# The startup's modulation in plain fp32, on four column tiles of the array

## The chip, the cores and the metric

The kernel runs on one core of a Trainium2 chip. The metric is device time in microseconds (us), from the first to the last instruction of the slowest core, here the only one; several runs are given by their median. The engines are PE (TensorE, matrix products), DVE (VectorE), ACT (ScalarE), POOL (GpSimd) and SP (SyncE, which here issues DMA transfers).

## What is computed

The program is a block of a hybrid model with three layers over 512 latent tokens and 256 context tokens, of width 2048. The change concerns the beginning of the first layer alone:

```python
shift_l, scale_l, gate_l = jnp.split(mod_lat, 3, axis=-1)
shift_c, scale_c, gate_c = jnp.split(mod_ctx, 3, axis=-1)
u_l = rms_norm(h_lat, pre_w) * (1 + scale_l[:, None]) + shift_l[:, None]
u_c = rms_norm(h_ctx, pre_w) * (1 + scale_c) + shift_c
z_l, xbc_l, dt_l, qkv_l, b_l, a_l = _split_proj(u_l @ w_in)
z_c, xbc_c, dt_c, qkv_c, b_c, a_c = _split_proj(u_c @ w_in)
```

`mod_lat` and `mod_ctx` are `silu(c) @ w_ada + b_ada` for two vectors of length 2048, one for the latent tokens and one for the context. Shift and scale are 4096 columns of `w_ada`, so 33.5 MB of weights are multiplied by two vectors only. The gate's columns are worked out elsewhere and are not touched.

## The kernel before, in words

Activations lie feature-major: 16 chunks of 128 features in the partitions, tokens in the columns. The large products run with split operands: a float32 value becomes a high part and a low part in a reduced format (`float32r`, F32R in the code), and three products (low weight by high activation, high by low, high by high) are added in PSUM. `gemm_steps` (L165 to L202) loads a block's weights four contraction chunks at a time (`wr`), converts them on ACT (`wh`, L183), subtracts on DVE (`wl`, L184), and issues the products at L198, contraction chunk by contraction chunk.

`startup` (L309) makes the input of the first layer. It has four inner steps:

- `modulation(k)` (L329) makes shift and scale of feature chunk k for both vectors. The stationary operand `c4` holds, for a contraction chunk, four columns: high and low parts of the two vectors. The moving operand is the weight, 128 x 256 for a contraction chunk (128 columns of shift, 128 of scale). It is loaded two contraction chunks at a time (`wa`, 256 KB, ten buffers), converted on ACT (`wah`, L336) and subtracted on DVE, every fourth time on POOL (`wal`, L337). So 32 products with a 4 x 256 result are added up in `pr` (L340). The sum is copied to `row` (ACT, L343), and two small fp32 products with `sel` (`pm`, L346) turn it into columns and add the parts; three DVE steps make `mod` (L350 to L352).
- `square(k)` (L355) loads chunk k of both streams (`raw`) and adds up their squares in `acc`.
- `rsqrt_rows` (L281) makes the norm's scale from `acc` (`rs`, L286).
- `modulate(k)` (L367) makes `u` on DVE (L372, L373) and splits it into `hi` (ACT, L274) and `xlo` (DVE, L275). These are the operands of all later products over chunk k.

`modulation(0)` and the sixteen squares come first; then, for each k, `modulation(k)` and `modulate(k)`. Beside them `phase_a` (L760) runs the first four blocks, over latent tokens (`mm`, 512 columns) and context (256 columns, shown as `s`): per chunk k these are 12 products of each kind, which can start when chunk k's `hi` and `xlo` are there.

The whole of this part is inside a block whose order a scheduler sets, from a model of its own; what it sets is a fixed order on each engine. Each engine, and SP's queue of transfers too, works it off strictly in that order. PSUM has two buffers for `pr`, `pm` and `rs` together while this runs.

Of the kernel before, what the change touches and what calls it, by code (L numbers as in the profile page):

```python
# [17 lines left out]
# products of other blocks between the dependent ones of the gated delta rule, by weight  # L18
# [4 lines left out]
# ---------------------------------------------------------------- layout on the host  # L23
# [107 lines left out]
# ---------------------------------------------------------------- the program  # L131
class Prog:
# [8 lines left out]
    # ---- constants  # L141
# [18 lines left out]
    # ---- products with split operands  # L160
# [4 lines left out]
    def gemm_steps(self, blocks, kc=16):  # L165
        """blocks: dicts of src [128, kc, M], acts [(hi, lo, psum ap)], done().  The blocks run
        together, contraction chunk by contraction chunk; a step is one matmul."""
# [36 lines left out]
    def gemm_tokens(self, src, done):  # L204
        """A product with the tokens in the partitions: src [128, 16, n], done(chunk of tokens, psum)."""
# [22 lines left out]
    def weave(self, steps, n, weight):  # L228
        """Steps of other products to place between dependent matmuls: n of them over the given weight."""
        self.steps, self.left, self.weight = steps, n, weight  # L230
# [10 lines left out]
    def run_slots(self, chain, other=None, skip=0, scale=1.0):  # L241
        """A chain of dependent products; between two of them a link of the other chain and steps of the filler."""
# [24 lines left out]
    # ---- small helpers  # L267
# [13 lines left out]
    def rsqrt_rows(self, acc, n, out, tmp):  # L281
        """out[p, t] = (sum_p acc[p, t] / n + eps) ** -0.5, the same in every partition."""
# [6 lines left out]
        # one table for both  # L289
# [3 lines left out]
        # one step of Newton's method  # L293
# [4 lines left out]
    def transposes(self, ps, dst, srcs):  # L298
        """PE transposes of srcs (each [a, b]) next to each other into one bank, one copy out."""
        nc = self.nc  # L300
        o = 0
        for s in srcs:
            a, b = s.shape
            nc.tensor.transpose(ps[:b, o:o + a], s, self.ident[:a, :a])
            o += a


    # ---- block 1, phase A: modulation, input projections of both streams, SSD, GDN preparation
    def startup(self):  # L309
        nc, D = self.nc, self.D  # L310
        self.xh, self.xl, self.ch, self.cl = [], [], [], []
        with self.tc.tile_pool(name="st", bufs=2, side="right") as st:
# [7 lines left out]
            nc.vector.tensor_scalar(out=cc, in0=cc, scalar1=0.5, scalar2=None, op0=MUL)  # L320
            # both vectors' high and low parts, next to each other as stationary columns
            c4 = st.tile([P, 16, 4], F32R, name="c4", bufs=1)
            nc.scalar.activation(out=c4[:, :, 0:2], in_=cc, func=AF.Copy)
            nc.vector.tensor_tensor(out=c4[:, :, 2:4], in0=cc, in1=c4[:, :, 0:2].bitcast(F32), op=SUB)  # L324
            sel = st.tile([4, 2], F32, name="sel", bufs=1)
            nc.vector.tensor_tensor(out=sel, in0=self.ident[0:4, 0:2], in1=self.ident[0:4, 2:4], op=ADD)
            xr, cr, R, mod = [], [], acc, st.tile([P, 16, 2, 2], F32, name="mod", bufs=1)

            def modulation(k):  # L329
                pr = self.sc("pr")  # L330
                for q in range(8):
                    w = st.tile([P, 2, 256], F32, name="wa", bufs=10)
                    nc.sync.dma_start(w, D["wada"][k, :, 2 * q:2 * q + 2])
                    wh = st.tile([P, 2, 256], F32R, name="wah", bufs=6)
                    wl = st.tile([P, 2, 256], F32R, name="wal", bufs=6)
                    nc.scalar.activation(out=wh, in_=w, func=AF.Copy)  # L336
                    (nc.gpsimd if q % 4 == 3 else nc.vector).tensor_tensor(out=wl, in0=w, in1=wh.bitcast(F32), op=SUB)  # L337
                    for j in range(2):
                        for i, x in enumerate((wl, wh)):
                            nc.tensor.matmul(pr[0:4, 0:256], c4[:, 2 * q + j, :], x[:, j, :],  # L340
                                             start=(q + j + i == 0), stop=(q + j + i == 9))
                row = st.tile([4, 256], F32, name="row")
                nc.scalar.activation(out=row, in_=pr[0:4, 0:256], func=AF.Copy)  # L343
# [11 lines left out]
            def square(k):  # L355
                # the streams wait in the places of their parts
# [24 lines left out]
            # the first modulations run beside the loads of the streams  # L381
# [13 lines left out]
    def conv_consts(self):  # L395
        """Half of the convolutions' taps and bias: silu(x) = (tanh(x / 2) + 1) * (x / 2)."""
# [22 lines left out]
    def conv5(self, ps, is_lat, taps, bias, out, th):  # L419
        """out = silu of the centred convolution of ps."""  # L420
# [20 lines left out]
    def both(self, src, done, share=None):  # L441
        """A block over the latent tokens and over the context."""
# [10 lines left out]
    def conv_block(self, names, j, has_bias, sink):  # L453
        """done() of a block that goes through a convolution; sink(out_lat, out_ctx)."""
# [16 lines left out]
    def small_done(self, ps, pc):  # L471
        """dt, beta and alpha of all tokens (context first): decays and their sums in each chunk."""
        nc, b1 = self.nc, self.b1
        with self.tc.tile_pool(name="sm", bufs=1, side="right") as st:
# [59 lines left out]
            # decay to the chunk's end times dt; minus the decay from the chunk's start  # L534
# [5 lines left out]
    # ---- SSD: units of four heads  # L540
# [3 lines left out]
    def ssd_bc(self, kind, lat, ctx):  # L544
        """B or C of a group: keep the feature-major latent part, B also token-major."""
# [12 lines left out]
    def to_tm(self, dst, lat, ctx, eng="act"):  # L558
        """dst[:, c, :] (token-major chunks) from feature-major latent and context parts."""
# [19 lines left out]
    def ssd_unit(self, u, xt):  # L579
        """Four heads; xt [tokens of a chunk, chunk, 256] holds their x."""  # L580
# [35 lines left out]
        # feature-major, to DRAM  # L616
# [40 lines left out]
    # ---- gated delta rule, preparation: everything that needs k and v alone  # L657
    def gdn_prep(self, h):
# [23 lines left out]
        # token-major k and its squared norms  # L682
# [19 lines left out]
        # token-major v over the norm of k  # L702
# [8 lines left out]
        # X[j, i] = k_j . k_i with the decay between j and i: forward above, backward below  # L711
# [9 lines left out]
        # its diagonal blocks of 32, rows scaled, lower triangular for both directions  # L721
# [16 lines left out]
    def gdn_solve(self, h, g, eng):  # L738
        """Inverses of the unit lower triangular 32-blocks of two heads, a block in a partition."""
# [6 lines left out]
        # in place: 2 on the diagonal turns the column of a step into its negative  # L746
# [13 lines left out]
    def phase_a(self):  # L760
# [74 lines left out]
        with tc.tile_pool(name="gp", bufs=1, side="right") as self.gp:  # L835
# [18 lines left out]
            # the first queries and gate, while the last preparations end  # L854
# [13 lines left out]
    # ---- gated delta rule: the inverses, the scans  # L868
    def gdn_data(self, h, hd):
        """What the scans of a head need."""  # L870
# [4 lines left out]
    def gdn_load(self, h):  # L875
        """The operands of the products for a head's inverses."""
# [35 lines left out]
    def gdn_merge(self, hd):  # L912
        """W = (I + D X)^-1 of every chunk (forward: upper, backward: lower), from its diagonal
        blocks; both directions share the products."""
# [11 lines left out]
        # 32 -> 64  # L926
# [13 lines left out]
        # 64 -> 128  # L940
# [17 lines left out]
    def gdn_step(self, h, hd, cs, S, tag, last=False):  # L958
        """One chunk of both directions' scans: the corrected values; the next states into S."""
# [47 lines left out]
    def gdn_lat(self, h, hd, qf, before):  # L1007
        """before: what takes the last head's outputs."""
# [11 lines left out]
        # squared norms of q  # L1020
# [34 lines left out]
        # the norms of q and of the outputs, token by token  # L1055
# [13 lines left out]
        return o  # L1069

    def zgate(self, ps, pool, pin=lambda ins: ins):
        """2 silu(z)."""
        nc = self.nc
        zs = pool.tile([P, 512], F32, name="zs")
        pin(nc.scalar.activation(out=zs, in_=ps, func=AF.Tanh, scale=0.5))
# [888 lines left out]
```

## Time and profile before

| | us |
|---|---|
| median of 3 runs | 3560.84 |
| lowest, highest | 3559.32, 3570.53 |
| span of the profiled execution | 3565.4 |

The time of the profiled execution is its span, 3565.4 us: one execution of its own, beside the three that were timed. The profile's views are: the page (busy time of each engine, and the span in slices); busy time by stretches of the span, with the granted TensorE clock as a share of full speed (1.00 is 2.4 GHz, 0.50 is 1.2 GHz) and the DMA engines' share; groups of instructions by line and shape, with count, busy time, mean of one in ns, and the engine's idle time just before them with what ended it; and instructions in order of time. A product in plain fp32 stands in the trace as two records of PE (and two weight loads, on the row PEld), one in `float32r` as one. The busy time of a record on PE goes on for a while after the next one has started, so that what a product occupies is read from start to start.

### The profile page before, as it was taken

The page shows a single profiled execution, that of the slowest core. Times are in us where ns is not written, and L with a number is a line of the kernel's source. Part 1 is how long each engine was busy: PE and PEld are TensorE (multiplying, and loading weights), DVE is VectorE, ACT ScalarE, POOL GpSimd, SP SyncE. Part 2 cuts the span into 40 slices and gives each one's busy share as a digit, 9 for nine tenths or more (in the row PEclk, how much of TensorE's full clock was granted, in tenths as well). Part 3 has the DMA queues.
Part 4 walks back from the last instruction along what each step waited for, and adds up shares of the span by engine and source line. Part 5 has one row for each costly group of instructions (what it writes and reads, how often), then busy time and mean ns, then how long its engine had stood idle before and what let it go on. Part 6 is the DMA issues. An engine that isn't in the chain of part 4 may idle for free.

```text
span 3565.4 us, 49253 instructions
## 1 busy us (share of the span) xinstructions
PE 3410.4 (96%) x17334; PEld 2843.3 (80%) x17334; DVE 2172.4 (61%) x4187; ACT 1511.4 (42%) x3036; POOL 543.6 (15%) x679
## 2 busy tenths in 40 slices
PE   5899999989999998999999999999999999999998
PEld 4688888878888786778888788887888888878887
DVE  7978776778865657666565634546444535353456
ACT  6554434444444435664333434434333333332334
POOL 4211114851110003202231201000000000000000
PEclk8999999999999999999999999999999999999999
DMA  8723336664443774333323454453333333345345
GB/s 272 239 78 108 92 83 215 205 193 133 126 127 94 231 250 137 101 113 95 98 83 98 116 183 136 136 149 107 107 105 101 101 102 102 89 132 156 96 123 170
DMA packets 293257, 479.79 MB, mean 135 GB/s; under 512 B 53689, under 2 KB 86841, under 8 KB 290833
## 3 DMA queue, kind: packets, MB, share of 16 engines
q1 hardware_dynamic: 293008, 476.65, 45.1%
q8 instruction: 136, 2.23, 0.3%
q14 instruction: 113, 0.92, 0.1%
HBM read 415.17 MB, written 61.34 MB: 134 GB/s over the span
## 4 chain that ended last, share of the span: by engine, by line
PE 72%; DVE 12%; DMA 7%; issue 3%; ACT 3%; POOL 2%; SPq 0%; DVEq 0%; ACTq 0%; POOLq 0%
PE mm L198 52%; PE mm L222 3%; PE mm L223 2%; PE mm L224 2%; PE mmc L198 2%; DVE wl L184 2%; DMA wg<-in_wgate 1%; PE pr L340 1%; DVE e L1570 1%; PE mg L922 1%; PE pl L198 1%; DMA araw<-yF 1%; ACT wh L183 1%; DVE at L1577 1%; PE s L198 1%
## 5 line engine op out<-in xcount | busy, mean ns | idle before, releaser
L198 PE MATMUL mm<-hi,wl 128*128 128x512 f32 (+2 forms) x3632 | 1414.7, 392 | 22.7 <-DVE wl L184 14.6
L198 PE MATMUL mm<-xlo,wh 128*128 128x512 f32 (+2 forms) x3632 | 1421.0, 391 | 6.4 <-DVE xlo L278 6.4
L198 PE MATMUL mm<-hi,wh 128*128 128x512 f32 (+2 forms) x3632 | 1415.1, 390 | 0.0
L184 DVE TENSOR_TENSOR wl<-wr,wh 128x512 fp32r<-128x512 f32 (+1 forms) x940 | 657.4, 705 | 687.0 <-ACT wh L183 683.1
L183 ACT ACTIVATE wh<-wr 128x512 fp32r<-128x512 f32 (+1 forms) x940 | 579.6, 621 | 1153.4 <-PE mm L198 908.0
L198 PEld LDWEIGHTS mm<-hi,wl 128*128 128x128 f32 (+1 forms) x3632 | 687.2, 190 | 149.2 <-DVE wl L184 19.9
L198 PEld LDWEIGHTS mm<-xlo,wh 128*128 128x128 f32 (+1 forms) x3632 | 686.6, 189 | 143.0 <-DVE xlo L278 8.7
L198 PEld LDWEIGHTS mm<-hi,wh 128*128 128x128 f32 (+1 forms) x3632 | 686.0, 189 | 122.8 <-issue 3.6
L222 PE MATMUL mm<-wl,hi 128*128 128x256 f32 (+1 forms) x512 | 172.3, 336 | 0.0
L223 PE MATMUL mm<-wh,xlo 128*128 128x256 f32 (+1 forms) x512 | 172.2, 336 | 0.0
L224 PE MATMUL mm<-wh,hi 128*128 128x256 f32 (+1 forms) x512 | 172.0, 336 | 0.0
L216 ACT ACTIVATE wh<-wr 128x512 fp32r<-128x512 f32 x96 | 60.6, 632 | 156.5 <-PE mm L224 77.7
L217 DVE TENSOR_TENSOR wl<-wr,wh 128x512 fp32r<-128x512 f32 x96 | 68.4, 714 | 88.9 <-ACT wh L216 88.4
L436 DVE SCALAR_TENSOR_TENSOR cvl<-padl,hc,cvl 128x512 f32<-128x512 f32 x112 | 91.8, 827 | 24.7 <-ACT cvl L432 15.5
L198 PE MATMUL mmc<-xlo,wh 128*128 128x256 f32 x368 | 106.0, 288 | 0.0
L222 PEld LDWEIGHTS mm<-wl,hi 128*128 128x128 f32 x512 | 97.2, 190 | 10.4 <-DVE pad L1349 0.3
L198 PE MATMUL mmc<-hi,wl 128*128 128x256 f32 x368 | 105.4, 286 | 0.0
L198 PE MATMUL mmc<-hi,wh 128*128 128x256 f32 x368 | 105.3, 286 | 0.0
L223 PEld LDWEIGHTS mm<-wh,xlo 128*128 128x128 f32 x512 | 97.2, 190 | 10.0
L224 PEld LDWEIGHTS mm<-wh,hi 128*128 128x128 f32 x512 | 97.2, 190 | 10.0
L340 PE MATMUL pr<-wal,c 128*4 128x256 f32 x256 | 69.4, 300 | 23.7 <-DVE c L324 10.6
L336 ACT ACTIVATE wah<-wa 128x512 fp32r<-128x512 f32 x128 | 74.5, 620 | 39.7 <-PE pr L340 23.7
(588 smaller groups left out, 4406.1 us busy)
## 6 DMA issues: line engine op xcount, KB each, us to landing
wr<-in_o_in SPq DMA_DIRECT2D x192, 256.0 KB, 3.1
wr<-in_e_in SPq DMA_DIRECT2D x160, 256.0 KB, 3.1
wr<-in_pgate SPq DMA_DIRECT2D x148, 256.0 KB, 3.3
wa<-in_wada SPq DMA_DIRECT2D x128, 256.0 KB, 4.2
wr<-in_w_qkv SPq DMA_DIRECT2D x96, 256.0 KB, 3.2
wr<-in_w_z SPq DMA_DIRECT2D x64, 256.0 KB, 3.1
wr<-in_w_out SPq DMA_DIRECT2D x64, 256.0 KB, 4.5
wg<-in_wgate SPq DMA_DIRECT2D x16, 1024.0 KB, 7.5
```

What stands on the lines that cost most here:

```text
L183: nc.scalar.activation(out=hi, in_=r, func=AF.Copy)
L184: nc.vector.tensor_tensor(out=lo, in0=r, in1=hi.bitcast(F32), op=SUB)
L198: nc.tensor.matmul(ap, w[:, kk, :], x, start=(n == 0), stop=(n == total[key] - 1))
L216: nc.scalar.activation(out=hi, in_=r, func=AF.Copy)
L217: nc.vector.tensor_tensor(out=lo, in0=r, in1=hi.bitcast(F32), op=SUB)
L222: nc.tensor.matmul(ps[c][:, :n], self.xh[k][:, t], lo[:, i], start=first, stop=False)
L223: nc.tensor.matmul(ps[c][:, :n], self.xl[k][:, t], hi[:, i], start=False, stop=False)
L224: nc.tensor.matmul(ps[c][:, :n], self.xh[k][:, t], hi[:, i], start=False, stop=last)
L336: nc.scalar.activation(out=wh, in_=w, func=AF.Copy)
L340: nc.tensor.matmul(pr[0:4, 0:256], c4[:, 2 * q + j, :], x[:, j, :], start=(q + j + i == 0), stop=(q + j + i == 9))
L436: nc.vector.scalar_tensor_tensor(out=ov, in0=pad[:, :, j:j + n], scalar=taps[j], in1=ov, op0=MUL, op1=ADD)
L922: nc.tensor.matmul(v[:, c], lhs[:, c], rhs[:, c], start=True, stop=True)
```

## The change

Inside `startup` only. Conversion and subtraction of the weights are left out, and with them `wah`, `wal` and the split of the two vectors. The vectors lie in `c32`, padded with zeros to 32 columns, in plain fp32. Weights are loaded four contraction chunks at a time (512 KB, ten buffers), and each of the four is multiplied in its own 32 columns of the array (`tile_position=(0, 32 * j)`), with its result in its own 32 partitions of `pr`. Per feature chunk there are 16 products with a 32 x 256 result. `row` then has 128 partitions, and `sel` adds the four partial sums: it has ones in rows 0, 32, 64 and 96 for the first vector, and in the rows after those for the second.

```diff
-            nc.vector.tensor_scalar(out=cc, in0=cc, scalar1=0.5, scalar2=None, op0=MUL)
-            c4 = st.tile([P, 16, 4], F32R, name="c4", bufs=1)
-            nc.scalar.activation(out=c4[:, :, 0:2], in_=cc, func=AF.Copy)
-            nc.vector.tensor_tensor(out=c4[:, :, 2:4], in0=cc, in1=c4[:, :, 0:2].bitcast(F32), op=SUB)
-            sel = st.tile([4, 2], F32, name="sel", bufs=1)
-            nc.vector.tensor_tensor(out=sel, in0=self.ident[0:4, 0:2], in1=self.ident[0:4, 2:4], op=ADD)
+            c32 = st.tile([P, 16, 32], F32, name="c32", bufs=1)
+            nc.gpsimd.memset(c32, 0.0)
+            nc.vector.tensor_scalar(out=c32[:, :, 0:2], in0=cc, scalar1=0.5, scalar2=None, op0=MUL)
+            sel = st.tile([P, 2], F32, name="sel", bufs=1)
+            s01 = st.tile([P, 2], F32, name="s01", bufs=1)
+            nc.vector.tensor_tensor(out=sel, in0=self.ident[:, 0:2], in1=self.ident[:, 32:34], op=ADD)
+            nc.vector.tensor_tensor(out=s01, in0=self.ident[:, 64:66], in1=self.ident[:, 96:98], op=ADD)
+            nc.vector.tensor_tensor(out=sel, in0=sel, in1=s01, op=ADD)
...
             def modulation(k):
                 pr = self.sc("pr")
-                for q in range(8):
-                    w = st.tile([P, 2, 256], F32, name="wa", bufs=10)
-                    nc.sync.dma_start(w, D["wada"][k, :, 2 * q:2 * q + 2])
-                    wh = st.tile([P, 2, 256], F32R, name="wah", bufs=6)
-                    wl = st.tile([P, 2, 256], F32R, name="wal", bufs=6)
-                    nc.scalar.activation(out=wh, in_=w, func=AF.Copy)
-                    (nc.gpsimd if q % 4 == 3 else nc.vector).tensor_tensor(out=wl, in0=w, in1=wh.bitcast(F32), op=SUB)
-                    for j in range(2):
-                        for i, x in enumerate((wl, wh)):
-                            nc.tensor.matmul(pr[0:4, 0:256], c4[:, 2 * q + j, :], x[:, j, :],
-                                             start=(q + j + i == 0), stop=(q + j + i == 9))
-                row = st.tile([4, 256], F32, name="row")
-                nc.scalar.activation(out=row, in_=pr[0:4, 0:256], func=AF.Copy)
+                for q in range(4):
+                    w = st.tile([P, 4, 256], F32, name="wa", bufs=10)
+                    nc.sync.dma_start(w, D["wada"][k, :, 4 * q:4 * q + 4])
+                    for j in range(4):
+                        nc.tensor.matmul(pr[32 * j:32 * j + 32, 0:256], c32[:, 4 * q + j, :], w[:, j, :],
+                                         start=(q == 0), stop=(q == 3), tile_position=(0, 32 * j))
+                row = st.tile([P, 256], F32, name="row")
+                nc.scalar.activation(out=row, in_=pr[:, 0:256], func=AF.Copy)
```

The scheduler sets the order anew. On PE, before, the products of a later modulation stand in pairs of low and high weights between those of the four blocks; here is the place behind a modulation's `pm` where the last of them are split up (`wal` and `wah` are the low and high weights, `c_109` the vectors, `s_...` the context's products):

```order
L198 MATMUL s_1959<-hi,wl 128x256
L340 MATMUL pr<-wal,c_109 4x256
L340 MATMUL pr<-wah,c_109 4x256
L340 MATMUL pr<-wal,c_109 4x256
L340 MATMUL pr<-wah,c_109 4x256
L198 MATMUL mm<-xlo,wh 128x512
```

And in the changed program, behind a `pm` near the same place (here L339 is the product and L345 `pm`):

```order
L345 MATMUL pm<-sel,row 128x2 x2
L339 MATMUL pr<-wa,c_108 32x256 x8
L198 MATMUL mm<-xlo,wh 128x512
L339 MATMUL pr<-wa,c_108 32x256 x4
L198 MATMUL mm<-hi,wh 128x512
L198 MATMUL s_1064<-xlo,wh 128x256
```

The products of a modulation now stand in groups of 4 to 16 between those of the blocks; over all sixteen modulations there are 27 such groups instead of 43.

On DVE, before, the subtractions stand between the steps of a chunk:

```order
L350 TENSOR_SCALAR mod<-pm,vec 128x2 x2
L372 TENSOR_TENSOR u<-raw,acc 128x256
L337 TENSOR_TENSOR wal<-wa,wah 128x512 x2
L352 TENSOR_SCALAR mod<-mod,vec 128x2
L337 TENSOR_TENSOR wal<-wa,wah 128x512
L373 TENSOR_SCALAR u<-u,mod 128x512
L373 TENSOR_SCALAR u<-u,mod 128x256
L337 TENSOR_TENSOR wal<-wa,wah 128x512
L275 TENSOR_TENSOR xlo<-u,hi 128x512
```

And in the changed program:

```order
L349 TENSOR_SCALAR mod<-pm,vec 128x2 x2
L351 TENSOR_SCALAR mod<-mod,vec 128x2
L372 TENSOR_SCALAR u<-u,mod 128x512
L372 TENSOR_SCALAR u<-u,mod 128x256
L275 TENSOR_TENSOR xlo<-u,hi 128x512
L275 TENSOR_TENSOR xlo<-u,hi 128x256
L371 TENSOR_TENSOR u<-raw,acc 128x512
L371 TENSOR_TENSOR u<-raw,acc 128x256
```

The steps that make `mod`, `u` and `xlo` of a chunk now follow each other directly.

## Rows read from the trace of the kernel before

**Rows 1.** The page: span, and busy time of each engine.
```profile
span 3565.4 us, 49253 instructions
PE 3410.4 (96%) x17334; PEld 2843.3 (80%) x17334; DVE 2172.4 (61%) x4187; ACT 1511.4 (42%) x3036; POOL 543.6 (15%) x679
```

**Rows 2.** Busy time by stretches (two answers of this view).
```profile
core 0: us, PE busy (x) PEld busy (x) DVE busy (x) ACT busy (x) POOL busy (x), PEclk, DMA share, GB/s
38.00:206.00 168.00, 150.80 (x930) 113.57 (x931) 144.90 (x251) 98.35 (x194) 50.20 (x42) 0.90 0.63 201
0.00:38.00 38.00, 7.67 (x37) 3.67 (x37) 22.64 (x36) 26.77 (x51) 17.91 (x28) 0.79 0.96 327
206.00:400.00 194.00, 190.27 (x1087) 166.25 (x1086) 160.71 (x361) 87.17 (x192) 26.49 (x30) 0.99 0.37 103
...
38.00:50.00 12.00, 8.66 (x44) 4.59 (x44) 10.67 (x14) 11.74 (x23) 4.75 (x4) 0.78 0.93 324
```

**Rows 3.** Order of time, PE, 60 to 84 us: start, length, instruction, count.
```profile
63.93 0.60 PE L346 MATMUL pm<-sel,row 4*128 4x2 f32 x4
64.46 0.28 PE L340 MATMUL pr<-wal,c 128*4 128x256 f32 x1
64.58 0.28 PE L340 MATMUL pr<-wah,c 128*4 128x256 f32 x1
...
73.06 0.39 PE L198 MATMUL mm<-xlo,wh 128*128 128x512 f32 x1
73.29 0.40 PE L198 MATMUL mm<-hi,wh 128*128 128x512 f32 x1
...
74.55 0.28 PE L198 MATMUL s<-hi,wh 128*128 128x256 f32 x1
74.67 0.28 PE L198 MATMUL s<-hi,wl 128*128 128x256 f32 x1
```

**Rows 4.** Groups by line and shape, 38 to 206 us.
```profile
L336 ACT ACTIVATE wah<-wa 128x512 fp32r<-128x512 f32 x120 | 69.4, 619 | 37.6 <-PE pr L340 23.7 <-issue 13.8
L337 DVE TENSOR_TENSOR wal<-wa,wah 128x512 fp32r<-128x512 f32 x90 | 65.1, 743 | 6.7 <-ACT wah L336 6.7
L340 PE MATMUL pr<-wah,c 128*4 128x256 f32 x240 | 63.4, 296 | 0.0
L340 PE MATMUL pr<-wal,c 128*4 128x256 f32 x240 | 63.4, 295 | 10.3 <-DVE wal L337 7.8 <-POOL wal L337 2.1 <-DVE sq L288 0.4
L337 POOL TENSOR_TENSOR wal<-wa,wah 128x512 fp32r<-128x512 f32 x30 | 48.3, 1612 | 103.9 <-ACT wah L336 97.1 <-DMA wa<-in_wada 6.8
...
L198 PE MATMUL mm<-hi,wl 128*128 128x512 f32 x65 | 21.1, 451 | 3.9 <-ACT hi L274 3.9
L198 PE MATMUL s<-xlo,wh 128*128 128x256 f32 x64 | 18.3, 292 | 0.8 <-DVE xlo L275 0.8
...
L275 DVE TENSOR_TENSOR xlo<-u,hi 128x512 fp32r<-128x512 f32 x16 | 17.4, 1086 | 3.2 <-ACT hi L274 2.9
...
L346 PE MATMUL pm<-sel,row 4*128 4x2 f32 x60 | 9.8, 265 | 2.2 <-DVE u L372 2.2
```

**Rows 5.** Order of time, PE, 37 to 62 us.
```profile
37.87 2.93 PE L286 MATMUL rs<-acc,ones 128*128 128x512 f32 x4 [16.41 <-DVE acc L365]
...
50.02 0.38 PE L340 MATMUL pr<-wal,c 128*4 128x256 f32 x1 [0.54 <-DVE wal L337]
50.20 0.41 PE L340 MATMUL pr<-wah,c 128*4 128x256 f32 x1
50.41 0.41 PE L340 MATMUL pr<-wal,c 128*4 128x256 f32 x1
```

**Rows 6.** Groups by line and shape: 300 to 3500 us, and PE over the span.
```profile
L275 DVE TENSOR_TENSOR xlo<-araw,hi 128x512 fp32r<-128x512 f32 x48 | 32.3, 687 | 18.2 <-ACT hi L274 18.2
...
L1025 PE MATMUL qn<-ones,sqq 128*128 128x1 f32 x64 | 7.6, 240 | 0.0
```

**Rows 7.** Order of time, all engines, 83 to 93 us.
```profile
87.03 3.91 POOL L337 TENSOR_TENSOR wal<-wa,wah 128x512 fp32r<-128x512 f32 x2 [5.08 <-ACT wah L336]
...
88.28 2.80 DVE L373 TENSOR_SCALAR u<-u,mod 128x512 f32<-128x512 f32 x2
...
88.41 0.28 PE L340 MATMUL pr<-wal,c 128*4 128x256 f32 x1 [0.66 <-DVE wal L337]
...
89.56 0.28 PE L340 MATMUL pr<-wal,c 128*4 128x256 f32 x1 [0.52 <-POOL wal L337]
```

**Rows 8.** Order of time, PE, 2508 to 2512 us: products in plain fp32, two records each.
```profile
2509.22 0.60 PE L1854 MATMUL nm<-vt,Wm 128*128 128x257 f32 x2
2509.65 0.59 PE L1860 MATMUL cm<-vt,kw 128*128 128x257 f32 x2
2510.09 0.60 PE L1856 MATMUL nm<-C,qg 128*128 128x257 f32 x2
```

**Rows 9.** Order of time, PE, 196 to 208 us.
```profile
199.84 2.07 PE L198 MATMUL mm<-hi,wl 128*128 128x512 f32 x4 [1.95 <-ACT hi L274]
...
202.14 0.63 PE L198 MATMUL mm<-xlo,wh 128*128 128x512 f32 x1
202.56 0.63 PE L198 MATMUL mm<-hi,wh 128*128 128x512 f32 x1
```

**Rows 10.** DMA queues, 38 to 206 us.
```profile
DMA packets 18534, 33.69 MB, mean 201 GB/s; under 512 B 2164, under 2 KB 2164, under 8 KB 18519
```

## The prediction

> **What bounds the kernel now.** I read the page first: PE is busy 96% of the span, nothing else over 61% [rows 1]. So the time moves by the work taken from PE or given to it, and by the idle time around it. The change touches only `startup`; with line and buffer numbers set aside, the order of the instructions after it is the same in both programs. So the second view is the busy time by stretches [rows 2]. The first 38 us belong to the DMA queues (share 0.96, 327 GB/s), and PE is busy 7.7 us in them. From 206 us on PE is busy 190.3 of 194 us at a granted clock of 0.99: whatever the startup ends earlier or later comes out at the end nearly whole. Between lies a stretch of 168 us (38 to 206) in which the 15 remaining modulations and the first four blocks' products run. There PE shows as busy 150.8 us, but at a mean clock of 0.90, and DVE is busy 144.9.
>
> What PE's work of that stretch is worth at the full clock I add up from starts in the order of time [rows 3]: a `pr` product each 0.116 us, a 512-column product each 0.23, a 256-column one each 0.116, the four records of `pm` 0.53. The groups [rows 4] give the counts: 480 x 0.116 = 55.7 for `pr`, 194 x 0.23 = 44.6, 192 x 0.116 = 22.3, 15 x 0.53 = 8.0, and 2.9 for the row sums `rs` [rows 5]. That is 133.5 of 168 us: **34.5 us are lost**. Idle before PE's groups makes 17.2 of it (10.3 + 3.9 + 2.2 + 0.8) [rows 4], and a clock 10% below full over 168 us makes 16.8, so the loss is accounted for. The low clock follows the idle: at 50.2 us, behind an idle 0.54, the same `pr` products start 0.21 us apart [rows 5], which is the 1.2 GHz level.
>
> Who causes the loss stands beside it. The 90 subtractions `wal` on DVE take 65.1 us, the 30 on POOL 48.3 [rows 4]. DVE's order puts them between the steps that turn a modulation into the next products' operands, and while POOL subtracts, DVE slows down: `xlo` of 128x512 has a mean of 1086 ns here against 687 later [rows 4, 6]. At 87 us POOL takes 3.91 us for two subtractions, two of DVE's `u` take 2.80 in the same time, and PE waits for both [rows 7].
>
> **The change, part by part.** The conversions `wah` (ACT, 120 in the stretch, 69.4 us) and the subtractions go away [rows 4]. They were on the path only where PE waited for them, so I count those waits and not their length. Loading stays 2 MB per chunk, in 64 transfers of 512 KB instead of 128 of 256. On SP the same 2 MB stand ahead of the stream's loads as before, so the squares and `rs` stay near 38 us: 0. The ten buffers now hold two and a half chunks instead of one and a quarter; the next weights of `w_xbc` queue behind them on SP, but are wanted only every four chunks: 0. The added memset (POOL) and the added sums for `sel` (DVE) lie before the first weights land: 0, and under 1 us without that cover. `row` keeps its 256 columns: 0. `pm` keeps two products, now over 128 rows instead of 4; fp32 records over 128 rows with one column have a mean of 240 ns, those of `pm` 265 [rows 4, 6]: 0.
>
> The `pr` products are the question. Per chunk, 32 one-record products become 16 in plain fp32, and the trace has no product in column tiles. The nearest are fp32 products of 257 columns over the whole array: two records each, one product every 0.43 to 0.44 us [rows 8]. From both sides: if the tiles share nothing, 240 x 0.435 = 104.4 us; if four run at once, a quarter, 26.1. I take the middle way, **two at once**: the two records of one product need the same columns of the array, and records start in program order [rows 8], so the second record of tile j can overlap only with the first of tile j+1. That is 0.2175 per product, 240 x 0.2175 = 52.2 us.
>
> Then the edges. The order has `pr` in 27 groups, 26 of them in this stretch. A group's last record runs alone: 26 x 0.22 = 5.7 us at least. If the array also has to empty on both sides, a record's length beyond the start of the next comes on top, 0.39 - 0.23 = 0.16 us [rows 3], twice: 26 x 0.54 = 14.0. I take the middle, 9.9. The Trainium skill ("TensorEngine Tiling (Array Packing)", Key Properties) says that changing the tiling mode drains TensorE, which speaks against the change; by it alone the edges cost the upper 14.0 and the gain below is 16 us. No row of this trace shows such a switch.
>
> So `pr` takes 52.2 + 9.9 = 62.1 instead of 55.7: PE gets 6.4 us more work. The gain must come from the 34.5 us lost. What stays: the slow clock of the first 12 us (0.78, 2.6 us) [rows 2], the wait for the last chunk's `hi` at 199.8 us (2.0) with the half clock after it (about 1.5) [rows 9], `xlo` 0.8, and about 1 for what is next in line, the chain `row`, `pm`, `mod`, `u`, `hi`, `xlo` of each chunk (some 3.5 us, covered by the next chunk's `pr` and the products of the chunk before). I keep 8. Gain: 34.5 - 8 - 6.4 = **20 us**; the startup ends at 186 instead of 206.
>
> DVE is no new bound: without `wal` it has 144.9 - 65.1 = 79.8 us, less without POOL beside it. DMA neither: 33.7 MB [rows 10], at the 327 GB/s of the first stretch are 103 us, done by 141.
>
> The sum is against the profiled execution, whose span is 3565.4 us; the median of the runs is 3560.84, 0.13% lower. I take the 20 us from the median: 3541.
>
> **Rivals.** *The tiles do not overlap* (slower). Then each product costs 0.435 and `pr` 104.4 + 26 x 0.16 for one emptying per group = 108.6, 52.9 more than now. With PE so full some 6 of the 34.5 stay lost: 52.9 - 28.5 = +24, 3585 us. It decides from the point where a chunk's `pr` costs, with its edges, 5.5 us instead of today's 3.7: 55.7 plus the 26.5 to be regained, over 15. My forecast has 62.1 / 15 = 4.1. For it: every fp32 product in the trace takes four times a split one, and no row shows two at once. Against: the tiles' outputs and weights are apart.
>
> *All four tiles run at once.* Then `pr` takes 26.1 + 9.9 = 36 us and PE is done after 77.8 + 36 + 8 = 122 us, at 160; the last weights land at 141, plus some 10 for the last chunk's chain and products. Both are close and will wait for each other a little: 160 to 166, a gain of 43, 3518 us. For it: four tiles, four outputs. Against: two records per product on the same columns. The Trainium skill ("TensorEngine Tiling (Array Packing)", Theoretical Speedup) gives up to 4 times for 32 columns, which would be this case.
>
> *Nothing to measure.* The second record also waits for its tile's weights to be loaded, so a chunk's `pr` costs 4.8 to 6.2 us with its edges and the regained waits pay for it: 15 x 0.7 = 10.5 us on either side of the point of decision above, 3550 to 3571.
>
> **How the numbers follow.** Two at once 0.50; none 0.23; four 0.15; in between 0.12. The measurement can tell about 0.3% from no change, 10.7 us. Of the first case a tenth falls within that, of the last most: faster 0.61, same 0.14, slower 0.25. The first case's own range is 3530 to 3552 (edges 5.7 to 14.0, kept losses 4 to 12, `rs` some us either way). To leave out no more than 2 in 10 the range must reach both other cases: 3516 to 3586.
>
> **What would show it.** Starts of consecutive `pr` records in the profile after: two records on the same start or at 0.11 us on average mean two tiles at once; 0.21 means none; 0.05 means four. The first four blocks' last 256-column products should end near 186 us; POOL nearly empty between 45 and 186; `xlo` of 128x512 near 690 ns; the granted clock there at 0.97 or more; no wait on `wal`. I am wrong if `pr` costs well over 4.1 us per chunk, or if PE keeps waiting though its work is the same: for `wa` from the DMA queues, or with the clock at the lower level inside the groups of `pr`.

## The result and the profile after

The change takes 3509.47 us, median of 4 runs (3507.06 to 3510.70), beside 3562.34 of the kernel before (3559.32 to 3570.53): ratio 0.9849, 95% interval 0.9837 to 0.9861. That is 52.9 us less. The prediction said 3541 in a range of 3516 to 3586: the sign is right, the size is not, and the range misses it. The profiled run has a span of 3508.2 against 3565.4 [rows 1].

The page after, its span and busy times. PE has 39 us less to do than in [rows 1], DVE 83, ACT 69, POOL 52:

```profile
span 3508.2 us, 48716 instructions
PE 3371.2 (96%) x17334; PEld 2813.7 (80%) x17334; DVE 2089.4 (60%) x4092; ACT 1442.6 (41%) x2907; POOL 491.2 (14%) x648
```

Where the startup ends shows where the time came from. The last `s` record starts at 205.5 us in the trace before and at 149.3 in that after, 56.2 earlier; the spans differ by 57.2. So nearly all of it lies ahead of that mark. The two records, first before, then after:

```profile
205.54 0.28 PE L198 MATMUL s<-hi,wh 128*128 128x256 f32 x1
```

```profile
149.27 0.28 PE L198 MATMUL s<-hi,wh 128*128 128x256 f32 x1
```

Busy time after, from the same 38 us to that mark, and the stretch of 194 us behind it, against [rows 2]:

```profile
core 0: us, PE busy (x) PEld busy (x) DVE busy (x) ACT busy (x) POOL busy (x), PEclk, DMA share, GB/s
38.00:149.50 111.50, 109.84 (x929) 80.37 (x928) 64.67 (x161) 34.10 (x72) 1.69 (x12) 1.00 0.80 298
149.50:343.50 194.00, 190.09 (x1064) 165.51 (x1063) 159.18 (x356) 84.81 (x188) 27.50 (x30) 0.97 0.37 101
```

As many records of PE (929 against 930) now lie in 111.5 us instead of 168, with 1.7 us of PE not busy where there were 17.2, and a mean granted clock of 1.00 where it was 0.90. DVE is busy 65 us instead of 145, POOL 1.7 instead of 50.

PE's groups of that stretch after, by line and shape (busy us, mean ns | idle before them), which answer to [rows 4]:

```profile
L339 PE MATMUL pr<-wa,c 128*32 128x256 f32 x480 | 32.0, 391 | 0.0
L198 PE MATMUL mm<-xlo,wh 128*128 128x512 f32 x64 | 26.2, 409 | 0.0
L198 PE MATMUL mm<-hi,wl 128*128 128x512 f32 x65 | 20.3, 401 | 0.6 <-ACT hi L274 0.6
L198 PE MATMUL s<-xlo,wh 128*128 128x256 f32 x64 | 18.0, 284 | 0.0
L345 PE MATMUL pm<-sel,row 128*128 128x2 f32 x60 | 7.6, 232 | 1.1 <-ACT row L342 1.1
```

The 480 `pr` records are 240 fp32 products of two records each. They were to cost 62.1 us and take 32.0. How they run shows in the order of time on PE after, some groups from 39 to 70 us (start, length, instruction, count); before stand [rows 3, 5]:

```profile
39.96 2.64 PE L339 MATMUL pr<-wa,c 128*32 128x256 f32 x32
...
47.56 0.50 PE L198 MATMUL mm<-xlo,wh 128*128 128x512 f32 x1
...
54.69 1.93 PE L339 MATMUL pr<-wa,c 128*32 128x256 f32 x32
56.55 0.39 PE L198 MATMUL s<-hi,wl 128*128 128x256 f32 x1
...
59.92 1.07 PE L339 MATMUL pr<-wa,c 128*32 128x256 f32 x16
60.93 0.50 PE L198 MATMUL mm<-xlo,wh 128*128 128x512 f32 x1
61.36 0.64 PE L339 MATMUL pr<-wa,c 128*32 128x256 f32 x8
61.93 0.50 PE L198 MATMUL mm<-hi,wh 128*128 128x512 f32 x1
```

From the first start of a group to the start of the next instruction, 32 records take 1.86 us, 16 take 1.00, 8 take 0.57: **0.432 us for four products (eight records), and 0.137 once per group**. The view groups like records, so the single starts of one group, read from the trace, stand here (us):

```
68.021 68.028 68.035 68.041 | 68.261 68.268 68.275 68.281 | 68.477 68.484 68.490 68.497 | 68.693 ...
```

Four records start within 20 ns, and 0.216 us later the next four: 0.054 on average. All four tiles run at once. These are the first records of the four products, then their four second records, since records of one tile start at least 0.216 apart in every run below.

The first 3.5 us of the window still run at half pace: `rs` takes 2.90 us, as long as before (2.93), and in the `x32` group at 39.96, which takes 2.64 us against 1.93 later, the starts of one tile are 0.427 us apart at first and 0.216 from 41.6 us on; the group at 44.24 runs at the later pace. (The view shows a granted clock of 1.00 from the first microsecond of this trace on, where the trace before shows 0.79 for the first 38 us [rows 2]. For these first microseconds I therefore go by starts.) Once the startup runs, PE shows no wait of note: 0.6 us for `hi`, 1.1 for `row`, both ahead of 46 us, and none for the DMA queues.

The other signs, in DVE's group after, 38 to 152 us, beside 1086 ns in [rows 4], and in the DMA queues of that stretch, beside [rows 10] (a digit is the share of one of 40 slices; below it GB/s):

```profile
L275 DVE TENSOR_TENSOR xlo<-u,hi 128x512 fp32r<-128x512 f32 x16 | 11.1, 692 | 5.2 <-ACT hi L274 5.2
```

```profile
DMA  9999999999589999999949999997796991000000
GB/s 414 405 410 398 408 408 408 410 397 398 207 234 369 355 362 395 417 411 401 359 128 231 395 346 406 413 411 277 234 341 201 285 353 64 0 0 0 0 1 6
DMA packets 10080, 33.23 MB, mean 292 GB/s; under 512 B 1228, under 2 KB 1228, under 8 KB 10068
```

The queues move 398 to 414 GB/s in the first 28 us, not 327, and the weights have landed near 135 us.

### The profile page after: what moved, and what is told of

Its sections match the earlier page's. It is cut to its first block, busy times and chain, and to the rows that moved or that the text cites. A ratio compares the mean times of both kernels' runs of the same rounds, so it can differ in the third digit from the quotient of the medians.

```text
span 3508.2 us, 48716 instructions
## 1 busy us (share of the span) xinstructions
PE 3371.2 (96%) x17334; PEld 2813.7 (80%) x17334; DVE 2089.4 (60%) x4092; ACT 1442.6 (41%) x2907; POOL 491.2 (14%) x648
## 4 chain that ended last, share of the span: by engine, by line
PE 74%; DVE 12%; DMA 6%; issue 3%; ACT 3%; POOL 2%; SPq 0%; ACTq 0%; DVEq 0%; POOLq 0%
PE mm L198 55%; PE mm L222 3%; PE mm L223 3%; PE mm L224 3%; DVE wl L184 2%; PE mmc L198 2%; DVE e L1569 1%; PE pl L198 1%; PE mg L921 1%; PE pr L339 1%; ACT wh L183 1%; PE s L198 1%; DMA E<-AA 1%; DMA qe<-EA 1%; DMA araw<-yF 1%
## 5 line engine op out<-in xcount | busy, mean ns | idle before, releaser
L1332 DVE TENSOR_TENSOR zh<-mm,Rh 128x512 f32<-128x512 f32 x64 | 44.2, 690 | 72.5 <-PE mm L198 72.5
L198 PEld LDWEIGHTS mmc<-xlo,wh 128*128 128x128 f32 x368 | 70.0, 190 | 15.7
```

Source lines behind the costliest of these rows:

```text
L198: nc.tensor.matmul(ap, w[:, kk, :], x, start=(n == 0), stop=(n == total[key] - 1))
L1332: self.nc.vector.tensor_tensor(out=t, in0=ps, in1=rows, op=MUL)
```

## The experiments

Two things changed together: PE's `pr` records run in less time, and DVE, POOL and ACT lost the split. **Theory A**: both matter, but most of the forecast's error is that four tiles overlap fully. Its rivals: the overlap is worth little and the relief of DVE and POOL everything; or the other way round; or the larger loads did it.

**Only one tile.** All products go to tile 0, one after the other.

```diff
-  nc.tensor.matmul(pr[32 * j:32 * j + 32, 0:256], c32[:, 4 * q + j, :], w[:, j, :],
-                   start=(q == 0), stop=(q == 3), tile_position=(0, 32 * j))
+  nc.tensor.matmul(pr[0:32, 0:256], c32[:, 4 * q + j, :], w[:, j, :],
+                   start=(q + j == 0), stop=(q + j == 6), tile_position=(0, 0))
...
```

`row` and `sel` shrink with it to 32 rows, and in the next run to 64.

> All products of a modulation in the first of the four column tiles; no split, loads and shapes as in the change. Theory A (both count: four tiles at once make the products cheap, and the removed split work takes away PE's waits): a product then costs 0.43 us, 240 of them 104 us instead of about 30, so the startup ends some 74 us later than in the change: about 3583 us, slower than before. Theory B (the gain is the removed work of DVE, ACT and POOL alone): within 10 us of the change, 3500 to 3520. Starts of pr records 0.21 us apart or more.

Measured: 3584.49 us (3578.99 to 3588.29), ratio 1.0063 (1.0046 to 1.0080). A full chunk on PE in its trace:

```profile
62.34 7.09 PE L339 MATMUL pr<-wa,c 128*32 128x256 f32 x32
```

7.02 us to the next instruction for 32 records, 0.216 apart one by one. Without overlap the change is slower than the kernel before, as the rival "the tiles do not overlap" had it (3585), and the relief of DVE and POOL does not save it.

**Two tiles.** Products 0 and 2 go to tile 0, products 1 and 3 to tile 1.

```diff
+  t = 32 * (j % 2)
-  nc.tensor.matmul(pr[32 * j:32 * j + 32, 0:256], c32[:, 4 * q + j, :], w[:, j, :],
-                   start=(q == 0), stop=(q == 3), tile_position=(0, 32 * j))
+  nc.tensor.matmul(pr[t:t + 32, 0:256], c32[:, 4 * q + j, :], w[:, j, :],
+                   start=(q == 0 and j < 2), stop=(q == 3 and j > 1), tile_position=(0, t))
...
```

> The same products alternate between two column tiles. Theory A: two records at once, 0.216 us a product, 240 products 52 us and a few us of edges, some 26 us more than the change: 3535 us. Theory B: 3500 to 3520.

Measured: 3526.37 us (3524.62 to 3528.18), ratio 0.9898 (0.9884 to 0.9913). Its chunk on PE, its `pr` group, and its stretch up to the last `s` (173.8 us):

```profile
64.81 3.65 PE L340 MATMUL pr<-wa,c 128*32 128x256 f32 x32
```

```profile
L340 PE MATMUL pr<-wa,c 128*32 128x256 f32 x480 | 55.5, 383 | 0.0
```

```profile
38.00:174.00 136.00, 135.03 (x929) 93.50 (x928) 66.75 (x162) 36.02 (x73) 1.64 (x12) 0.99 0.69 244
```

This is the pace that I forecast: pairs 0.216 apart. `pr` takes 55.5 us, about what it took before (55.7), and still the kernel is 36 us faster, not 20. So the forecast would have been wrong by 15 us even with its own overlap: the rest of its sum was too dear as well.

**Tile by tile.** The four tiles stay, but a tile gets its four products in a row instead of one product per tile in turn.

```diff
-  nc.tensor.matmul(pr[32 * j:32 * j + 32, 0:256], c32[:, 4 * q + j, :], w[:, j, :],
-                   start=(q == 0), stop=(q == 3), tile_position=(0, 32 * j))
+  nc.tensor.matmul(pr[32 * q:32 * q + 32, 0:256], c32[:, 4 * q + j, :], w[:, j, :],
+                   start=(j == 0), stop=(j == 3), tile_position=(0, 32 * q))
```

> Four column tiles as in the change, but the products stand tile by tile: four in a row on one tile, then four on the next. If records start strictly in the order of the program, only the border between two tiles overlaps: 16 x 0.43 less 3 x 0.216, 6.3 us a chunk instead of 2.0, 3570 to 3575 us. If PE takes records of other tiles ahead, as the change's trace might also be read: 3505 to 3515.

Measured: 3564.62 us (3558.42 to 3568.39), ratio 1.0001 (0.9992 to 1.0011), between the two times expected. A group of one tile runs serially, and one of four tiles takes 4.59 us, neither 7.1 nor 1.9:

```profile
62.49 1.91 PE L339 MATMUL pr<-wa,c 128*32 128x256 f32 x8
...
73.75 4.59 PE L339 MATMUL pr<-wa,c 128*32 128x256 f32 x32
```

The trace does not name a record's tile, but the 32 starts of the last group fall into four series of eight, 0.216 apart; the eighth of each raises a semaphore, as the last product of a piece of weights does, so each series is one tile (us):

```
73.745 73.985 74.201 74.417 74.633 74.849 75.065 75.280
74.639 74.879 75.095 75.310 75.526 75.742 75.958 76.174
75.532 75.772 75.988 76.204 76.420 76.635 76.851 77.067
76.425 76.665 76.881 77.097 77.313 77.529 77.745 77.960
```

The second tile starts at 74.639, 6 ns behind the first tile's fifth record, while three of the first tile's records, all earlier in the program, still wait (74.849, 75.065, 75.280). The third and fourth tiles start in the same way. So a record for a free tile passes waiting records of a busy one, and in every series up to three of them. In the order of the change the fourth tile's first record has just three waiting ahead of it, the second records of tiles 0 to 2, and passes them too (68.041 before 68.261 above). What the text ahead of the prediction says of every engine, that it works off its order strictly, does not hold for products in different column tiles on PE. The Trainium skill ("TensorE: Matmul & The Clock Gate", Part 3: Packing small matmuls, The mechanism) says that matmuls start and end in program order without reordering. This trace differs: the first tile's last product, earlier in the program, starts at 75.065, 0.43 us behind the second tile's first one.

**No subtractions.** The kernel before without its `wal`.

```diff
-  wl = st.tile([P, 2, 256], F32R, name="wal", bufs=6)
-  (nc.gpsimd if q % 4 == 3 else nc.vector).tensor_tensor(out=wl, in0=w, in1=wh.bitcast(F32), op=SUB)
-  for i, x in enumerate((wl, wh)):
+  for i, x in enumerate((wh, wh)):
```

> The kernel before without the subtractions on DVE and POOL; the 32 products of a modulation all take the high part of the weights, so that PE and ACT have the work of before. It leaves out the weights' low parts and counts the high ones twice. Theory A: PE's 34 us of loss go, its 55.7 us of products stay: startup ends near 175 us, total near 3535. Theory B (the removed work is everything): near 3510. Theory C (PE's cheaper products are everything): 3550 to 3562.

Measured: 3537.90 us (3534.84 to 3541.02), ratio 0.9931 (0.9916 to 0.9946). PE's stretch up to its last `s` (182.0 us), and its `pr` group:

```profile
38.00:182.00 144.00, 139.67 (x928) 109.17 (x929) 68.27 (x162) 95.52 (x195) 1.60 (x4) 0.97 0.70 233
```

```profile
L338 PE MATMUL pr<-wah,c 128*4 128x256 f32 x480 | 61.6, 282 | 0.1
```

The same 480 one-record products, and 23.5 us less of the stretch: DVE and POOL held it, as the prediction said. ACT's conversions are all there (ACT busy 95.5 us), so they held little: 10.5 us stay lost here, 5.7 in the change (the table below).

**The split kept beside the change.** The conversions and subtractions run on as before, and nobody reads them.

```diff
+  for i in range(2):
+      wh = st.tile([P, 2, 256], F32R, name="wah", bufs=2)
+      wl = st.tile([P, 2, 256], F32R, name="wal", bufs=2)
+      nc.scalar.activation(out=wh, in_=w[:, 2 * i:2 * i + 2], func=AF.Copy)
+      e = nc.gpsimd if (2 * q + i) % 4 == 3 else nc.vector
+      e.tensor_tensor(out=wl, in0=w[:, 2 * i:2 * i + 2], in1=wh.bitcast(F32), op=SUB)
```

> The change, but the conversions on ACT and the subtractions on DVE and POOL run as before, with results that nobody reads (96 on DVE, 32 on POOL, 128 on ACT). Theory A (DVE and POOL were what PE waited for): DVE gets 65 us back into a stretch of 111 us in which it is now busy 65, and slows down beside POOL, so it becomes the bound: startup ends 20 to 40 us later, 3525 to 3550 us. If the gain were PE's cheaper products alone, nothing changes: 3505 to 3515.

Measured: 3554.66 us (3551.61 to 3566.56), ratio 0.9985 (0.9975 to 0.9996). DVE's busy time in its stretch, and who PE waits for:

```profile
62.00:92.00 30.00, 28.21 (x230) 20.01 (x228) 30.00 (x58) 19.27 (x37) 10.63 (x6) 1.00 0.67 226
```

```profile
PE pr L345 <- DMA wa<-in_wada: 16.3, 13, 2.4
PE mm L198 <- ACT hi L274: 4.8, 3, 3.4
PE pm L351 <- ACT row L348: 4.2, 3, 3.2
```

And who SP's queue waits for before it can issue the weights' loads (L337), from 38 to 192 us:

```profile
SPq L337 <- DVE wal L343: 59.0, 47, 3.0
SPq L337 <- POOL wal L343: 41.3, 24, 3.5
```

Slower than I expected. Between 62 and 92 us DVE is never idle; the subtractions hold the weight buffers, SP waits 59.0 us for those of DVE and 41.3 for those of POOL, so the next loads come late and PE waits 16.3 us for them. PE's work is nearly as short as in the change, and yet 50 of the 56 us that the change gains on this chip (3504.75 beside 3560.94, below) are gone. These copies have two buffers each instead of six, so a part of that may be theirs.

**Loads of half the size.** 256 KB per transfer in 20 buffers.

```diff
-  for q in range(4):
-      w = st.tile([P, 4, 256], F32, name="wa", bufs=10)
-      nc.sync.dma_start(w, D["wada"][k, :, 4 * q:4 * q + 4])
+  for q in range(8):
+      w = st.tile([P, 2, 256], F32, name="wa", bufs=20)
+      nc.sync.dma_start(w, D["wada"][k, :, 2 * q:2 * q + 2])
...
+          t = 32 * ((2 * q + j) % 4)
...
```

> The change with the weights in transfers of 256 KB as before, in twenty buffers of half the size (same bytes in flight); products on the same tiles. If the rate of the queues depends on the size (about 410 GB/s with 512 KB, 330 to 355 with 256 KB), 33 MB take some 95 to 100 us from 38 us on instead of 81; PE needs until 149 us, so little of it shows: 3508 to 3516. If the larger transfers were what fed PE: 3520 or more.

Measured: 3519.48 us (3513.78 to 3522.06), ratio 0.9876 (0.9861 to 0.9891): 14.7 us behind the change on the same chip (3504.75). From 38 to 62 us its queues move less than those of the change (first line here, then the change), but PE does not wait for them. What it pays in the startup is on PE:

```profile
38.00:62.00 24.00, 23.32 (x154) 12.60 (x155) 13.67 (x32) 9.01 (x18) 0.72 (x1) 1.00 1.03 373
```

```profile
38.00:62.00 24.00, 22.34 (x192) 14.06 (x190) 15.12 (x38) 9.13 (x18) 0.49 (x1) 1.00 1.03 408
```

```profile
L340 PE MATMUL pr<-wa,c 128*32 128x256 f32 x480 | 40.1, 399 | 0.0
```

```profile
55.82 0.62 PE L340 MATMUL pr<-wa,c 128*32 128x256 f32 x4
56.68 0.63 PE L340 MATMUL pr<-wa,c 128*32 128x256 f32 x4
```

A piece of weights now holds two products, and 20 of its 36 groups are of two products alone. They fill only two tiles and take 0.556 us to the next instruction, as long as four products (0.569). Neither theory had this: the load's size sets how many tiles one group can fill. It does not explain all: the last `s` starts at 158.7, 9.7 behind the change on the same chip (149.0), and of these `pr` makes 6.6 (table below). Some 5 us more of the time lie behind the startup, and no run shows their cause.

**Large loads alone.** The kernel before with 512 KB per transfer in 5 buffers.

```diff
-  w = st.tile([P, 2, 256], F32, name="wa", bufs=10)
-  nc.sync.dma_start(w, D["wada"][k, :, 2 * q:2 * q + 2])
+  if q % 2 == 0:
+      w4 = st.tile([P, 4, 256], F32, name="wa", bufs=5)
+      nc.sync.dma_start(w4, D["wada"][k, :, 2 * q:2 * q + 4])
+  w = w4[:, 2 * (q % 2):2 * (q % 2) + 2]
```

> The kernel before with its split weights, subtractions and one-record products kept, and only the weight loads made as large as in the change: 512 KB per transfer in 5 buffers instead of 256 KB in 10, so the same bytes are held. Theory A (the transfers of 512 KB raise the rate of the weight queue, but the startup before is held by the subtractions on DVE and POOL and by the order of PE behind them, so a faster queue gives nothing): 3556 to 3568 us, last s record at 203 to 207 us as before, DVE busy as much as before in 38 to 206. Theory B (the startup before is held by the rate of the weight loads): the rate goes from some 327 to some 400 GB/s, worth up to 20 us: 3538 to 3550 us.

Measured: 3557.70 us (3552.65 to 3563.79), ratio 0.9991 (0.9982 to 1.0001), last `s` at 202.6. The larger transfers alone give nothing that can be told from no change. The change also holds twice the bytes in its buffers (ten of 512 KB); no run takes that apart.

**Squares first, then the norm first.** Two tries to go on from the change by starting `rs` earlier. The first puts the sixteen squares ahead of the first modulation:

```diff
+  for j in range(16):
+      square(j)
   for k in range(ahead):
       modulation(k)
-      for j in range(16 * k // ahead, 16 * (k + 1) // ahead):
-          square(j)
```

> The change with the sixteen squares before the first modulation, so that the 2 MB of its weights are loaded behind the streams, while the norm is worked out. Row sums about 5 us earlier (near 32 instead of 37), the first products near 42 instead of 46 us: 3504 to 3507. If the adding up of squares (1.07 us a chunk on POOL) sets the time and not the loads: as the change, 3508 to 3511.

Measured: 3514.77 us (3512.83 to 3515.90), ratio 0.9866 (0.9850 to 0.9883). A miss, 10.0 us behind the change on the same chip: `rs` still stands behind the first chunk on PE, whose weights now come later:

```profile
32.80 2.26 PE L339 MATMUL pr<-wa,c 128*32 128x256 f32 x16 [32.80 <-DMA wa<-in_wada]
...
39.01 2.91 PE L286 MATMUL rs<-acc,ones 128*128 128x512 f32 x4
```

The last `s` starts at 151.7, only 2.7 later than in the change; the rest lies behind the startup, again without a cause that a run shows.

The second issues every modulation behind the norm:

```diff
-  ahead = 1
-  for k in range(ahead):
-      modulation(k)
-      for j in range(16 * k // ahead, 16 * (k + 1) // ahead):
-          square(j)
+  ahead = 0
+  for j in range(16):
+      square(j)
```

> The change with the squares and the row sums ahead of every modulation (nothing of a modulation is issued before them), so that on PE the row sums rs stand ahead of pr(0) and pm(0) instead of behind them. The second try of what squares_first missed. If the start is held by rs waiting for acc behind the first chunk's weights: the stream's loads come 2 MB (some 5 us at 410 GB/s) earlier, rs goes out near 32 instead of 36.8 us, but pr(0) comes later, since its weights are behind the stream: 3500 to 3505 us beside the change again on the same chip. If the weights bound the whole startup instead (298 GB/s mean and full queue to about 140 us), the order of the first loads moves nothing: within 2 us of the change again, last s record at 148 to 150.

Measured: 3507.28 us (3504.56 to 3510.27), ratio 0.9848 (0.9834 to 0.9861). `rs` does go out earlier, and what was hidden ahead of it now follows it:

```profile
32.37 2.90 PE L286 MATMUL rs<-acc,ones 128*128 128x512 f32 x4 [32.37 <-DVE acc L364]
35.27 2.92 PE L339 MATMUL pr<-wa,c 128*32 128x256 f32 x32
39.02 0.61 PE L345 MATMUL pm<-sel,row 128*128 128x2 f32 x4 [0.82 <-ACT row L342]
```

The 4.7 us that `rs` gains are spent on one more chunk's `pr` and `pm` behind it (35.27 to 39.55), which in the change run while PE waits for `rs`. The last `s` starts at 150.1, in the change on this chip at 149.4. No version here beats the change on its own chip.

**The change again**, on the chips of the second and third set of runs.

> The change itself on the same chip, for the comparison with squares_first and the others of this call: 3506 to 3513.

> The change once more, beside norm_first on the same chip: 3503 to 3511 us.

Measured: 3504.75 (3502.42 to 3505.23), ratio 0.9836 (0.9821 to 0.9850), and 3503.82 (3502.90 to 3510.91), ratio 0.9846 (0.9833 to 0.9860): 56.2 and 56.1 us less than the kernel before on the same chips. The last `s` starts at 149.0 and 149.4, as in the first trace (149.3); behind it these two traces are shorter than the first by 7.2 and 6.6 us.

**Together.** For each kernel: the time from 38 us to the start of its last `s` record; PE's `pr` at the full clock (groups and counts from its trace, 0.216 per step and some 0.13 per group, or 0.116 per old product; tile by tile and half-size loads by their starts); the other products (44.4 `mm` + 22.3 `s` + 6.5 `pm` + 2.9 `rs` = 76.1, before 77.8); and what is left, which is lost to idle time and a low clock.

| kernel | stretch | `pr` | others | lost |
|---|---|---|---|---|
| before | 167.5 | 55.7 | 77.8 | 34.0 |
| before, no subtractions | 144.0 | 55.7 | 77.8 | 10.5 |
| change, split kept | 153.6 | 30.7 | 76.1 | 46.8 |
| change, one tile | 186.1 | 105.4 | 76.1 | 4.6 |
| change, two tiles | 135.8 | 54.1 | 76.1 | 5.6 |
| change, tile by tile | 166.5 | 84.1 | 76.1 | 6.3 |
| change, half-size loads | 120.7 | 36.1 | 76.1 | 8.5 |
| change | 111.3 | 29.5 | 76.1 | 5.7 |

The two parts do not add up singly. With the split work there, shorter products only make PE wait longer for it (46.8 lost). Without it, every microsecond of `pr` shows in the stretch, and with loads of 512 KB 4.6 to 6.3 us stay lost whatever `pr` costs. The change removes 26.2 us of `pr`, 28.3 of loss and 1.7 of others: 56.2. One thing no run holds fixed: the scheduler sets the order anew for each kernel (`pr` stands in 26 groups in the stretch of the change, in 28 without subtractions, in 35 with the split kept).

## Why the prediction was wrong

Its method held: the span behind the startup differs by 1.0 us between before and after, and what the startup ended earlier came out at the end. (That remainder is not a constant: it differs by 7 us among three traces of the change.) Its sum for the stretch was 147.9 us (77.8 + 62.1 + 8); the trace after has 111.3. Step by step:

- **The step that failed**: "the two records of one product need the same columns of the array, and records start in program order, so the second record of tile j can overlap only with the first of tile j+1", hence two at once and 52.2 us. The first half agrees with the 0.216 us between records of one tile; the second is wrong. Records of free tiles pass waiting ones, and four run at once: 60 x 0.432 = 25.9 us, 26.3 less than forecast. [Rows 8] could not tell: there each product uses the whole array, so starts in order show no rule about tiles. The rule came from rows in which it had no chance to fail.
- **The edges**: 9.9 us forecast, bounds 5.7 to 14.0. Measured are 26 x 0.137 = 3.6, below the lower bound, which had the last record of a group run alone; here the last records of all four tiles run together. The Trainium skill's drain at a change of mode ("TensorEngine Tiling (Array Packing)", Key Properties) may be in the 0.137; no run here shows it apart. The edges do not cost the 14.0 that the prediction worked out beside it.
- **The kept losses**: 8 us against 5.7. The wait for the last chunk's `hi` [rows 9], 2.0 us and 1.5 of half clock behind it, is gone: 0.6 us, at 45.9, is all that PE waits for `hi`.
- **`pm`**: put at 0 change; its four records take 0.43 us instead of 0.53, 1.5 us over 15 chunks.
- **The price of two at once** was wrong by itself. With that overlap the run gives 3526, not 3541: its edges and losses are 54.1 - 51.8 = 2.3 and 5.6 us, where I had 9.9 and 8, and its stretch is 135.8 where the sum was 147.9. With all four tiles the rival's 3518 had the same 9.9 us of edges, and let the weights bound the end at 327 GB/s. They began at 398 to 414 and were not waited for.
- **Right**: the loss and its cause. Taking the subtractions away alone gives 25 us at unchanged products; `xlo` went to 692 ns, POOL is nearly empty, the granted clock is 1.00, and the conversions on ACT held at most the 4.8 us between 10.5 and 5.7.
- **Right, the last digits by luck**: the rival without overlap. 3585 forecast, 3584.5 measured with one tile; but its sum for the stretch, 108.6 + 77.8 + 6 = 192.4 us, is 6.3 above the 186.1 measured.
- **Loads**: put at 0, and larger transfers are worth that alone (0.9991). Not at 0 is what they make possible: with half the size, 20 groups fill two tiles only.

The chance stood wrong with it: 0.15 for four at once, against 0.50 for two. No row of the profile before spoke for two over four.

## What to carry to other kernels

Where a kernel pays other engines to split an operand so that TensorE runs one record instead of two, count both sides: narrow products in separate column tiles can win TensorE's side back, and the engines that did the splitting are relieved as well; each alone was worth far less than the two. Issue the products round the tiles, one per tile in turn, and let one load bring enough of them to fill all tiles: the same products tile by tile were 55 us slower (3564.6 against 3509.5). And when a forecast needs an ordering rule, ask whether the rows that seem to show it could have shown anything else.

## What the runs showed of the hardware

- Four fp32 products of 256 columns in four 32-column tiles take as long as one: 0.432 us for four, in one tile 0.43 each. This agrees with the up to 4 times of the Trainium skill ("TensorEngine Tiling (Array Packing)", Theoretical Speedup). Starts of the four lie 7 ns apart.
- A record passed up to three earlier, waiting records of another tile (74.639 before 74.849, 75.065 and 75.280). Whether it could pass more was not tried.
- A group of `pr` records between products over the whole array took 0.137 us beyond its products here, the same for groups of 8, 16, 24 and 32 records. How much of it is the change between column tiles and the whole array, no run shows.
- With weight loads of 512 KB the queues moved 408 GB/s between 38 and 62 us, with 256 KB 373. PE waited for the weights in neither.
